# A hybrid attention encoder on one core: the weight sums of x's first chunk in order of use

## The chip, the cores and the metric

The kernel runs on one core of a Trainium2 chip. The metric is the device time of one execution in microseconds (us), the median of several runs. Lower is better.

## The reference, cut to what matters

Two encoder layers on 512 tokens of width 1024, all in float32. Each layer normalizes x, makes one wide projection, runs attention over the tokens and over 256 memory tokens, gates the result and projects it back:

```python
for i in range(DEPTH):
    h = rmsnorm(x, norm_g[i])
    mem_h = rmsnorm(mem, mem_norm_g[i])
    proj = jnp.einsum('bsd,de->bse', h, w_in)          # w_in_a or w_in_b
    ...
    o_mem = memory_attention(q_mem, mem_h, w_mem_kv[i], mem_qn_g[i], mem_kn_g[i])
    y = jnp.concatenate([o_mix, o_mem], axis=-1) * jax.nn.silu(gate)
    x = x + jnp.einsum('bse,ed->bsd', y, w_out[i])
```

Nearly all the work is in the projections, whose weights (some 140 MB with the parts that are read twice) stream in from HBM.

## The kernel before, in words

**The products.** A large projection is cut into *chunks* of weight columns, and each chunk is computed by a Winograd form of Strassen's scheme: seven products instead of eight, at the price of sums of activation blocks and of weight blocks. Each product takes one or two weight tiles of 128x1024 (the index `x` in the code). In the order in which TensorE uses them (`ORDER`) the weight operands of a chunk are `21`, `11`, `T1`, `T2`, `22`, `T3`, `T4`. `21`, `11` and `22` are loaded as they are. The four sums are made on the chip: T1 = `12` + `11`, T2 = `22` + T1, T3 = `12` + `22`, T4 = `21` + T2.

**From a loaded tile to a product.** SyncE issues the loads (`Weights.dma`, L265), as many ahead as the budget of live tiles (`KEEP`, `KEEP_C`) lets it. The sums are drawn in `Weights.sum`. T1 is a VectorE add (L283) for most chunks; for the chunks that `by_dma` names, of which x's first chunk (index 0 in `PLAN`, the first that multiplies the normalized x; two chunks of memory keys and values come before it) is the one that matters here, it is a DMA issued by GpSimd that reads `11` again from HBM and adds it into the tile (L279). T2 (L288), T3 (L293) and T4 (L298) are adding DMAs from GpSimd too; T2 and T4 add one SBUF tile to another, T3 adds `22` from HBM. Products of float32 are made of three products of a rounded high part and a low part: ScalarE casts the high part `wh` (L314), VectorE subtracts for the low part `wo` (L324), and TensorE runs L174 and L175 with `wh` and L178 with `wo`. The operand ring holds four tiles.

**What sets the order.** The program's order is fixed while it is recorded. After each group of matmuls `Weights.advance` counts `g` up by one, records the subtractions, then draws at most one sum, the casts and the loads. `sum` goes through the first eight of its list, which stands in `ORDER`, and draws the first that is *ripe*: its load and the sum that it needs were recorded at least `LEAD` = 2 groups ago (one for some). A sum that isn't ripe is passed over. T1 of x's first chunk is also held back until `g` is `T1_AT` = 7. An engine works strictly in its recorded order: a DMA issue on GpSimd whose load hasn't landed holds all that stands behind it on GpSimd.

**What else stands in these queues.** GpSimd makes the factors of the norms: L495, L453 and L454 turn sums of squares into `rstd`, L663 scales it for the memory keys (`mem_kv`). VectorE multiplies with them (L604 makes `xn`, L500 normalizes x), TensorE transposes the products (L611, L506; L1096 for the memory queries of chunk 3). In `setup` SyncE loads the rope tables (L980 to L983, of which `grA` is a small one), VectorE scales them (L985 to L989), GpSimd multiplies them out (L992). Results leave PSUM by L389 (ScalarE) and L406 (VectorE); those of chunk 0 are stored by L1067 to `v0d`. Chunk 3 follows chunk 0, then chunk 4.

Of the kernel before, what the change touches and what calls it, by code (L numbers as in the profile page):

```python
# [24 lines left out]
BULK, ACTIVE, SET_AT, T1_AT, MEM_B, PREP_Y, PREP_B, HALF, SET_B = 2, 2, 15, 7, 14, 1, 1, {"a": 3, "b": 3, "o": 0}, 9  # L25
# [104 lines left out]
def trunk_kernel(ctx: ExitStack, tc: tile.TileContext, x, mem, wall, norm_g, mem_norm_g, gcol,  # L130
# [63 lines left out]
    def by_dma(c):  # L194

        return c == T1_DMA[0] or c >= T1_DMA[1]

    class Weights:
        def __init__(self):
            self.items, self.last, self.need, self.allocs, self.sums = [], [], [], [], []  # L200
            self.users, self.kinds = {}, []
            g = 0
            for c in SEQ:
                kind, d = PLAN[c], sum(pieces(k) for k in PLAN[:c])
                base = len(self.items)
                if kind in GROUPS:
# [20 lines left out]
                else:  # L227
# [3 lines left out]
                    for k in ORDER:  # L231
                        for x in range(n):
# [7 lines left out]
                            g += 1  # L240
                self.kinds += [kind] * (g - len(self.kinds))
            assert sum(pieces(k) for k in PLAN) == wall.shape[0]
            self.g = -1
            self.live = 0
# [25 lines left out]
        def sum(self, force=False, want=None):  # L270

            for n, (key, d) in enumerate(self.sums[:8]):
                if want and key != want:
                    continue
                c, k, x = key
                if k == "T1" and by_dma(c):
                    if not self.ripe(self.load_at, key, force) or self.g < T1_AT and not force:
                        continue
                    G.dma_start(self.tile[key], wall[d], accum_op=ALU.add)  # L279
                elif k == "T1":  # L280
                    if not (self.ripe(self.load_at, key, force) and self.ripe(self.at, (c, "11", x), force)):
                        continue
                    V.tensor_tensor(self.tile[key], self.tile[key], self.tile[c, "11", x], ALU.add)  # L283
                    self.use((c, "11", x))
                elif k == "T2":
                    if not (self.ripe(self.load_at, key, force) and self.ripe(self.at, (c, "T1", x), force, 1 if c < T1_DMA[1] else None)):
                        continue
                    G.dma_start(self.tile[key], self.tile[c, "T1", x], accum_op=ALU.add)  # L288
                    self.use((c, "T1", x))
                elif k == "T3":  # L290
                    if not self.ripe(self.load_at, key, force):
                        continue
                    G.dma_start(self.tile[key], wall[d], accum_op=ALU.add)  # L293
                else:
                    if not (self.ripe(self.lo_at, (c, "21", x), force, 1) and self.ripe(self.at, (c, "T2", x), force, T4_AT.get(c))):
                        continue
                    self.tile[key] = self.tile[c, "21", x]
                    G.dma_start(self.tile[key], self.tile[c, "T2", x], accum_op=ALU.add)  # L298
                    self.use((c, "T2", x))
                self.at[key] = self.g  # L300
                self.sums.pop(n)
                return True
            return False
# [1362 lines left out]
```

## Time and profile before

| | before |
|---|---|
| median of 3 runs | 959.22 us (958.16 to 960.2) |
| the profiled execution: its own time | 958.25 us |
| its span in the trace | 956.5 us |
| TensorE busy | 940.2 us (98%) |
| VectorE, ScalarE, GpSimd busy | 788.8, 679.6, 339.3 us |
| DMA: moved, mean rate | 204.55 MB, 214 GB/s |
| granted TensorE clock, mean | 0.996 |

TensorE's busy time is near the span, so the other engines matter where TensorE waits for them. In the page's rows, `L12` is line 12 of the kernel, `out<-in` are the program's names for tiles (`wl` a weight tile, `wh` and `wo` its high and low part, `pj` a PSUM tile), and the bracket at a row's end is the idle time of the engine before it and who ended it. A DMA issue appears on the engine that issues it (POOL is GpSimd, SPq is SyncE's queue); its transfer goes on afterwards on the 16 DMA engines, which all queues share.

### The profile page before, as it was taken

What the parts mean: (1) busy time and instruction counts of PE and PEld (TensorE: products, weight loads), DVE (VectorE), ACT (ScalarE), POOL (GpSimd) and SP (SyncE); (2) the same over time, 40 slices, a digit from 0 to 9 for tenths busy, and PEclk for the clock granted to TensorE, in tenths of its full rate; (3) what the DMA queues carried; (4) which work ended last, traced back from release to release, by engine and by line L of the source; (5) the groups of instructions that cost most, each with busy time, mean ns of one, the idle gap of its engine ahead of it and who ended that gap; (6) DMA issues with size and microseconds to landing.
All of it is one profiled execution on the core that took longest, in us unless ns stands there. A gap on an engine that the chain in (4) does not pass through costs nothing.

```text
span 956.5 us, 16572 instructions
## 1 busy us (share of the span) xinstructions
PE 940.2 (98%) x5680; PEld 833.1 (87%) x5680; DVE 788.8 (82%) x1411; ACT 679.6 (71%) x1696; POOL 339.3 (35%) x486
## 2 busy tenths in 40 slices
PE   8799999999999999999999999999899999999998
PEld 6688988888888888888889998888899999998886
DVE  6599676788888897979788999877988898779982
ACT  7565689786868676777676668547778977878860
POOL 3323422647454646373746111213232340111110
PEclk9899999999999999999999999999999999999999
DMA  9999936969786969696877979979966687786524
GB/s 349 362 248 322 290 114 162 311 133 253 158 262 155 263 156 255 147 244 144 228 184 199 278 195 249 288 239 317 245 156 133 194 233 181 206 206 184 119 61 129
DMA packets 86486, 204.55 MB, mean 214 GB/s; under 512 B 25089, under 2 KB 34561, under 8 KB 86402
## 3 DMA queue, kind: packets, MB, share of 16 engines
q1 hardware_dynamic: 66962, 139.46, 42.6%
q0 software_dynamic: 18144, 61.87, 34.9%
q10 hardware_dynamic: 1296, 2.16, 0.6%
q8 instruction: 45, 0.74, 0.3%
q14 instruction: 39, 0.32, 0.1%
HBM read 157.52 MB, written 11.34 MB: 177 GB/s over the span
## 4 chain that ended last, share of the span: by engine, by line
PE 89%; DMA 4%; DVE 3%; ACT 2%; issue 1%; POOL 1%; SPq 0%; DVEq 0%; POOLq 0%; ACTq 0%
PE pj L175 23%; PE pj L174 23%; PE pj L178 23%; PE qT L611 2%; DMA wl<-in_wall_dram 2%; PE sa L1186 1%; PE oo L1294 1%; PE pt L1273 1%; PE ptb L1496 1%; PE sa L1182 1%; DVE wo L324 1%; DMA x<-in_x_dram 1%; PE ob L178 1%; PE ob L175 1%; PE ob L174 1%
## 5 line engine op out<-in xcount | busy, mean ns | idle before, releaser
L324 DVE TENSOR_TENSOR wo<-wl,wh 128x1024 fp32r<-128x1024 f32 x255 | 315.7, 1244 | 6.0 <-ACT wh L314 5.7
L314 ACT CAST wh<-wl 128x1024 fp32r<-128x1024 f32 x255 | 268.6, 1060 | 33.3 <-PE pj L175 19.2
L174 PE MATMUL pj<-wh,hS 128*128 128x512 f32 (+1 forms) x448 | 157.4, 365 | 0.8 <-DVE sn L406 0.8
L175 PE MATMUL pj<-wh,hS 128*128 128x512 f32 (+1 forms) x448 | 152.3, 353 | 0.6 <-DVE hS L575 0.6
L174 PE MATMUL pj<-wh,h 128*128 128x512 f32 (+1 forms) x336 | 118.9, 367 | 0.0
L175 PE MATMUL pj<-wh,h 128*128 128x512 f32 (+1 forms) x336 | 115.2, 356 | 1.1 <-DVE h L575 1.1
L454 POOL TENSOR_TENSOR rstd<-mse,half 128x4 f32<-128x4 f32 (+2 forms) x96 | 101.3, 1056 | 8.0
L178 PE MATMUL pj<-wo,hS 128*128 128x512 f32 (+1 forms) x448 | 100.1, 353 | 0.0
L175 PEld LDWEIGHTS pj<-wh,hS 128*128 128x128 f32 x448 | 85.0, 190 | 11.1 <-DVE hS L575 0.8
L174 PEld LDWEIGHTS pj<-wh,hS 128*128 128x128 f32 x448 | 84.8, 189 | 11.1 <-DVE sn L406 1.2
L178 PEld LDWEIGHTS pj<-wo,hS 128*128 128x128 f32 x448 | 74.6, 189 | 12.2 <-DVE wo L324 0.4
L453 POOL TENSOR_SCALAR mse<-hss 128x4 f32<-128x4 f32 (+1 forms) x86 | 43.2, 503 | 112.1 <-ACT junk L599 107.8
L599 ACT ACTIVATE junk<-sn 128x128 f32<-128x128 f32 x264 | 79.1, 308 | 2.2 <-DVE sn L400 2.2
L389 ACT COPY sn<-pj 128x512 f32<-128x512 f32 x116 | 64.5, 590 | 21.6 <-PE pj L178 20.8
L1130 POOL TENSOR_TENSOR ta<-sn,tabs 128x128 f32<-128x128 f32 (+1 forms) x64 | 35.4, 561 | 118.2 <-DVE sn L604 91.2
L178 PE MATMUL pj<-wo,h 128*128 128x512 f32 (+1 forms) x336 | 75.6, 355 | 0.0
L175 PEld LDWEIGHTS pj<-wh,h 128*128 128x128 f32 x336 | 64.3, 191 | 8.9 <-DVE h L575 1.3
L174 PEld LDWEIGHTS pj<-wh,h 128*128 128x128 f32 x336 | 64.2, 191 | 7.4
L406 DVE TENSOR_TENSOR sn<-pj,sn 128x512 f32<-128x512 f32 x87 | 59.6, 686 | 8.5 <-PE pj L178 8.1
L298 POOL DMA_DIRECT2D wl<-wl x33 | 29.2, 896 | 104.4 <-DVE wo L324 49.4
L178 PEld LDWEIGHTS pj<-wo,h 128*128 128x128 f32 x336 | 56.6, 191 | 9.0
L288 POOL DMA_DIRECT2D wl<-wl x33 | 30.9, 960 | 66.3 <-DMA wl<-in_wall_dram 11.4
(252 smaller groups left out, 2361.3 us busy)
## 6 DMA issues: line engine op xcount, KB each, us to landing
wl<-in_wall_dram SPq DMA_DIRECT2D x222, 512.0 KB, 7.3
wl<-wl POOLq DMA_DIRECT2D x66, 512.0 KB, 5.6
wl<-in_wall_dram POOLq DMA_DIRECT2D x44, 512.0 KB, 8.5
od<-o SPq DMA_DIRECT2D x11, 256.0 KB, 5.4
og<-od SPq DMA_DIRECT2D x10, 256.0 KB, 8.6
x<-in_x_dram SPq DMA_DIRECT2D x4, 512.0 KB, 9.0
v0d<-sn SPq DMA_DIRECT2D x8, 256.0 KB, 6.0
acc<-in_x_dram POOLq DMA_DIRECT2D x8, 256.0 KB, 6.1
```

Source lines behind the costliest of these rows:

```text
L174: T.matmul(o, a, b, start=start, stop=False, skip_group_check=True)
L175: T.matmul(o, c, d, start=False, stop=False, skip_group_check=True)
L178: T.matmul(o, a, b, start=False, stop=stop, skip_group_check=True)
L288: G.dma_start(self.tile[key], self.tile[c, "T1", x], accum_op=ALU.add)
L314: A.copy(wh, self.tile[self.items[i]])
L324: V.tensor_tensor(wo, self.tile[key], wh.bitcast(F32), ALU.subtract)
L389: A.copy(t, b)
L406: V.tensor_tensor(t, b, t, ALU.subtract if q == "12" else ALU.add)
L453: G.tensor_scalar(e, ss, EPS, None, ALU.add)
L454: G.tensor_tensor(r, e, half[:, 0:n], ALU.pow)
L599: A.activation(jk, p[:, j * 128:(j + 1) * 128], AF.Square, scale=by, accum_out=ss[:, j:j + 1])
L1130: G.tensor_tensor(ta[:, 0:n], xn[:, 0:n, 0:32], ropeA[:, 0, b, s0:s0 + n], ALU.mult)
```

## The change

```diff
                 c, k, x = key
                 if k == "T1" and by_dma(c):
-                    if not self.ripe(self.load_at, key, force) or self.g < T1_AT and not force:
+                    if self.g < T1_AT and not force:
+                        break
+                    if not self.ripe(self.load_at, key, force):
                         continue
                     G.dma_start(self.tile[key], wall[d], accum_op=ALU.add)
```

While T1 of x's first chunk is held back (`g` below 7), the search now ends there, and nothing behind it in the list is drawn. Before, T1 was passed over and T3, whose load was old enough, was drawn ahead of it. The last chunks that `by_dma` names come long after `g` = 7, so nothing changes there. All line numbers behind the change are two higher.

What moves is small. On GpSimd, at the end of the memory keys and the beginning of chunk 0, there stood before (L495, L453, L454 is the norm of x's fourth block, L663 the factor of the second block of memory keys, L293 T3's sum, L279 T1's, L288 T2's, L298 T4's):

```order
L454 TENSOR_TENSOR rstd<-mse,half 128x4
L293 DMA wl<-in_wall_dram 128x1024
L495 TENSOR_TENSOR mse<-ss 128x1
L453 TENSOR_SCALAR mse<-mse 128x1
L454 TENSOR_TENSOR rstd<-mse,half 128x1
L663 TENSOR_SCALAR rstd<-rstd,rm 128x4
L293 DMA wl<-in_wall_dram 128x1024
L279 DMA wl<-in_wall_dram 128x1024 x2
L288 DMA wl<-wl 128x1024 x2
L298 DMA wl<-wl 128x1024 x2
```

And now:

```order
L456 TENSOR_TENSOR rstd<-mse,half 128x4
L497 TENSOR_TENSOR mse<-ss 128x1
L455 TENSOR_SCALAR mse<-mse 128x1
L456 TENSOR_TENSOR rstd<-mse,half 128x1
L665 TENSOR_SCALAR rstd<-rstd,rm 128x4
L281 DMA wl<-in_wall_dram 128x1024 x2
L290 DMA wl<-wl 128x1024 x2
L295 DMA wl<-in_wall_dram 128x1024 x2
L300 DMA wl<-wl 128x1024 x2
```

T3's two issues went from ahead of and between the norm's factors to behind T2's. On VectorE one instruction moves, in the second half of chunk 0's products: the add of chunk 3's T1 (L283). There stood before, between the low parts (L324) and the activation's low parts (L575):

```order
L324 TENSOR_TENSOR wo<-wl,wh 128x1024
L283 TENSOR_TENSOR wl<-wl 128x1024
L324 TENSOR_TENSOR wo<-wl,wh 128x1024
L575 TENSOR_TENSOR h_717<-f_478,h_717 128x4x128
L575 TENSOR_TENSOR hS_666<-fS_589,hS_666 128x4x128
L324 TENSOR_TENSOR wo<-wl,wh 128x1024 x2
L575 TENSOR_TENSOR h_717<-f_555,h_717 128x4x128
```

And now:

```order
L326 TENSOR_TENSOR wo<-wl,wh 128x1024 x2
L577 TENSOR_TENSOR h_715<-f_476,h_715 128x4x128
L577 TENSOR_TENSOR hS_664<-fS_587,hS_664 128x4x128
L326 TENSOR_TENSOR wo<-wl,wh 128x1024
L285 TENSOR_TENSOR wl<-wl 128x1024
L326 TENSOR_TENSOR wo<-wl,wh 128x1024
L577 TENSOR_TENSOR h_715<-f_553,h_715 128x4x128
```

The add went behind two more low parts of chunk 0 and two of the activation. TensorE, ScalarE and SyncE keep their order.

## Prediction

> **What bounds the kernel now.** I read the page first. TensorE is busy nearly all the time, and the DMA engines are full for the first five slices (some 120 us) and then nearly idle for one.
>
> ```profile
> span 956.5 us, 16572 instructions
> PE 940.2 (98%) x5680; PEld 833.1 (87%) x5680; DVE 788.8 (82%) x1411; ACT 679.6 (71%) x1696; POOL 339.3 (35%) x486
> DMA  9999936969786969696877979979966687786524
> ```
>
> So the end is set by TensorE's own stream, and only a stop of TensorE is worth anything. The timeline of TensorE over the first 130 us has one such stop; these are the rows around it (start, length, engine, line).
>
> ```profile
> 33.38 0.60 PE L611 MATMUL qT<-ident,xn 128*128 128x128 f32 x4
> 35.68 1.08 PE L178 MATMUL pj<-wo,act 128*128 128x512 f32 x4
> 42.80 1.09 PE L611 MATMUL qT<-ident,xn 128*128 128x128 f32 x4 [6.04 <-DVE xn L604]
> 47.10 1.83 PE L178 MATMUL pj<-wo,h 128*128 128x512 f32 x4
> 57.81 0.39 PE L174 MATMUL pj<-wh,hS 128*128 128x512 f32 x1
> ```
>
> TensorE waits 6.04 us for VectorE's xn (the last row, the first product with T1's weights, is used below). The timelines of VectorE and GpSimd say who held that up.
>
> ```profile
> 30.02 0.08 DVE L491 DVE_READ_ACCUMULATOR2_ANT ss<- 128x1 f32 x1
> 41.96 0.69 DVE L604 TENSOR_TENSOR xn<-pj,rstd 128x512 f32<-128x512 f32 x1 [9.33 <-POOL rstd L663]
> 29.67 1.33 POOL L454 TENSOR_TENSOR rstd<-mse,half 128x4 f32<-128x4 f32 x1
> 39.34 1.07 POOL L293 DMA_DIRECT2D wl<-in_wall_dram  x1 [8.34 <-DMA wl<-in_wall_dram]
> 40.18 0.47 POOL L495 TENSOR_TENSOR mse<-ss 128x1 f32<-128x1 f32 x1
> 41.62 0.30 POOL L663 TENSOR_SCALAR rstd<-rstd,rm 128x4 f32<-128x4 f32 x1
> 42.52 2.07 POOL L279 DMA_DIRECT2D wl<-in_wall_dram  x2
> ```
>
> GpSimd was free at 31.0 (29.67 + 1.33) and the input of L495 was there at 30.1, but L293, the issue of T3's first sum, stood in front and waited for its load until 39.3. The whole chain L495 to L663, then VectorE, then TensorE, stood behind it.
>
> **What the change removes.** In the changed order GpSimd has no DMA issue before L663. L495 to L663 takes 41.92 - 40.18 = 1.74 us, so L663 ends at about 31.0 + 1.8 = 32.8, not 41.9, and xn at 33.5. TensorE ends its group at 36.76 (35.68 + 1.08), so it doesn't wait: 6.04 us go. There is a second part. The windows give the granted clock:
>
> ```profile
> 36.70:42.80 6.10, 0.06 (x2) 0.04 (x1) 0.84 (x2) 1.97 (x3) 3.29 (x7) 0.92 1.04 390
> 42.80:49.00 6.20, 6.20 (x19) 4.99 (x20) 6.11 (x9) 0.81 (x2) 1.79 (x2) 0.53 1.06 219
> 43.20:48.00 4.80, 4.80 (x15) 3.85 (x14) 4.80 (x7) 0.00 (x0) 1.39 (x2) 0.50 1.06 208
> 71.00:75.00 4.00, 4.00 (x20) 3.30 (x19) 4.00 (x5) 3.92 (x6) 0.00 (x0) 1.00 0.76 225
> 85.00:107.00 22.00, 22.00 (x179) 21.60 (x178) 17.80 (x19) 12.08 (x29) 4.29 (x5) 1.00 1.05 341
> 126.00:144.00 18.00, 18.00 (x104) 15.75 (x103) 14.02 (x23) 15.08 (x45) 4.78 (x8) 1.00 0.23 65
> ```
>
> (The last three columns are granted clock, DMA share, GB/s.) The clock falls late in the stop, and TensorE then runs at 0.53 for 6 us. A transpose and its group took 36.76 - 33.38 = 3.38 us before the stop and 48.93 - 42.80 = 6.13 after it: 2.75 us more. So TensorE gets 6.04 + 2.75 = **8.8 us** ahead by about 40 us.
>
> **What the sums that move cost.** T1's two issues (L279) no longer stand behind T3's and can start at 32.8 instead of 42.5; T2's follow, and T3's come after them. The nearest row to their need is this wait of ScalarE for T2's second sum:
>
> ```profile
> 63.64 1.05 ACT L314 CAST wh<-wl 128x1024 fp32r<-128x1024 f32 x1 [2.52 <-DMA wl<-wl]
> ```
>
> With TensorE 8.8 us early it is needed at 54.9. The chain from the first L279 to that landing lasted 63.6 - 42.5 = 21.1 us; from 32.8 it ends at 53.9. It is in time, by 1 us. Loads now share the engines with the chain, so a delay of 0 to some 3 us is possible; I take none. T3's sums are used after T2's (the order of use is 21, 11, T1, T2, 22, T3, T4), and VectorE's add for chunk 3 (L283) moves behind two low parts of 1.2 us and two shorter ones; its own use comes much later, and I take nothing for either.
>
> **What is late next.** This decides the sum. The share of 1.04 to 1.06 in the windows means that the DMA engines have no free time; only 71 to 75 us shows a gap, 4 x (1 - 0.76) = 1.0 us. The change moves no byte away. So whatever waited for a landing in before between 77 and 124 us cannot get it more than about 1 us earlier, however early TensorE is. Three places wait in order for such landings.
>
> First, VectorE's L989 needs the small table grA.
>
> ```profile
> grA<-in_qn_a_dram SPq DMA_DIRECT2D x1, 48.0 KB, 8.5
> 65.98 0.42 SPq L982 DMA_DIRECT2D grA<-in_qn_a_dram  x1
> 69.16 0.86 POOL L288 DMA_DIRECT2D wl<-wl  x1 [4.16 <-DVE wl L283]
> 69.75 1.17 POOL L293 DMA_DIRECT2D wl<-in_wall_dram  x1
> 77.21 0.20 DVE L989 TENSOR_SCALAR grA<-grA 128x96 f32<-128x96 f32 x1
> 77.93 5.34 DVE L324 TENSOR_TENSOR wo<-wl,wh 128x1024 fp32r<-128x1024 f32 x2
> 85.32 1.23 DVE L283 TENSOR_TENSOR wl<-wl 128x1024 f32<-128x1024 f32 x1 [2.05 <-DMA wl<-in_wall_dram]
> 86.46 1.22 DVE L324 TENSOR_TENSOR wo<-wl,wh 128x1024 fp32r<-128x1024 f32 x1
> 84.45 1.07 PE L178 MATMUL pj<-wo,h 128*128 128x512 f32 x4
> 90.15 1.12 PE L178 MATMUL pj<-wo,h 128*128 128x256 f32 x8
> ```
>
> The table landed at 65.98 + 8.5 = 74.5. Behind the change, chunk 3's two sums, which GpSimd issued at 69.2 and 69.8, come earlier (the first waits for VectorE's L283, which follows TensorE's pace, less those four VectorE instructions) and get in front of it. A sum moves 0.524 MB at the 208 GB/s of the window 43.2 to 48, where sums run alone: 2.5 us each. So the table lands between 73.5 (the gap of 1.0 used, no sum ahead) and 79.5 (both ahead, no gap used); I take 77.4, nearer to both ahead, less the gap and about 1 us of overlap. VectorE would reach L989 at 77.2 - 8.8 = 68.4 and then stand there until 77.4, about when it got there before. Half of the 5.34 us pair after it is T4's second low part, ready at about 80.8; TensorE used it at 84.45. So TensorE keeps 84.45 - 80.8 = 3.7 us and gives back 5 us in a new wait there.
>
> Second, L283 (chunk 4's first sum) waited for loads that landed at 85.3. Landing 1.0 us earlier, its successor L324 ends at 86.7 instead of 87.7, against TensorE's use at 90.15: 3.5 us stay.
>
> Third, GpSimd at 105 us.
>
> ```profile
> 105.42 0.93 POOL L293 DMA_DIRECT2D wl<-in_wall_dram  x1 [6.71 <-DMA wl<-in_wall_dram]
> 107.12 0.88 POOL L293 DMA_DIRECT2D wl<-in_wall_dram  x1 [0.76 <-DMA wl<-in_wall_dram]
> 108.38 1.05 POOL L454 TENSOR_TENSOR rstd<-mse,half 128x4 f32<-128x4 f32 x1
> 109.47 0.69 DVE L604 TENSOR_TENSOR sn<-sn,rstd 128x512 f32<-128x512 f32 x1 [2.60 <-POOL rstd L454]
> 111.65 0.60 PE L1096 MATMUL qT<-ident,sn 128*128 128x128 f32 x4
> ```
>
> This is the same blockade again, with chunk 4's T3: rstd stands behind L293. VectorE's product ends at 110.16 and TensorE uses it at 111.65, 1.5 us later. With landings 1.0 us earlier, TensorE can keep 1.5 + 1.0 = **2.5 us**. After 126 us the DMA share is 0.23, nothing waits for landings, and what is left should last to the end.
>
> The sum, against the profiled execution of 958.25 us: -8.8, then +5.1 at T4's second low part, +0.2 at L283, +1.0 at L293, so -2.5: 955.75. The median of the three runs is 959.22, 0.97 above the profiled run; so I forecast **956.7**.
>
> **Rivals.** (B) *The clock falls at the new stop.* The removed stop of 6.0 us cost 2.75 us of slow clock; the new one of about 5 us may cost the same. TensorE then keeps 3.7 - 2.75 = 0.95 us, below what GpSimd at 105 us allows: 958.3. For it: the two stops are nearly as long. Against it: the old clock fell only in the last part of the stop (0.92 on average over it), and part of the new stop may be spread over earlier small waits. The Trainium skill, page "TensorE: Matmul & The Clock Gate", section "What's actually happening", says that the clock halves after one idle window of about 3.4 us, and that the window runs freely. By that rule a stop of 5 us halves it in about half of the cases (an estimate from the page: (5.0 - 3.4)/3.4), which would give 958.3 in those and 956.7 in the others; the two windows of 0.92 and 0.53 agree with it.
>
> (C) *More comes through.* If the sums do not get in front of the loads, the table lands at 73.5 and chunk 4's loads 2.5 to 5 us earlier; -4 to at most -8.8: 950.4 to 955.2. Against it speaks the full DMA share over 85 to 107 us.
>
> (D) *Slower: sums overtake loads.* If one more sum of 2.5 us (chunk 3's last, L298) is served before the loads for L283 and no gap is used, L283 starts at 87.8, its L324 ends at 90.2, and TensorE, which used it at 90.15, has gained nothing; the longer stop, over 6 us, also brings 2.75 us of slow clock: 962.0. It decides from a landing at about 86 us on, with the clock down. For it: the sums do move forward in time against the loads. Against it: L298 stands behind the rope table's products on GpSimd, which themselves wait for grA.
>
> **How the numbers follow.** A measurement of this kernel can tell about 0.2%, 1.9 us, from no change. My forecast has 0.45 (of it 0.38 beyond 0.2%), B 0.25 (0.22 within, 0.03 slower by its spread), C 0.12 (all faster), D 0.18 (0.17 slower, 0.01 within). So faster 0.50, same 0.30, slower 0.20. The range 951.5 to 961.5 leaves out the far end of C and the worst of D, less than 0.2 together. The forecast's own range is 955.5 (all 3.7 us stay) to 957.7 (no landing earlier at all, 1.5 us stay).
>
> **What would show it.** Right: TensorE has no wait at 36 to 43 us, and GpSimd's rstd chain (now L497 to L665) ends near 32.8; the group of T1 starts near 49 us instead of 57.8; VectorE idles at the table grA (now L991) for several us and TensorE waits at T4's second low part between 75 and 81 us; GpSimd's L295 ends its wait near 104; TensorE's transpose L1098 stands near 109. A granted clock of about 0.5 in the windows after 80 us means B. Wrong: if the grA table has landed before 72 us or T1's group isn't early, the step on landings or the step on the chain has failed; if VectorE waits at L285 beyond 86 us, it is D.

## The result, and the profile after

| | before | after |
|---|---|---|
| median | 959.0 us (958.02 to 960.24, 15 runs) | 957.83 us (956.68 to 959.4, 15 runs) |
| ratio, 95% interval | | 0.9987 [0.9979, 0.9995] |
| profiled execution, span | 958.25 us, 956.5 us | 958.09 us, 956.2 us |

The changed kernel is 1.2 us faster, 0.13%. The forecast was 956.7 us (0.26%); 957.83 lies in its wide range, and just outside its own range of 955.5 to 957.7.

The page of the changed kernel shows the same instructions and almost the same busy times; only the time between them moved.

```profile
span 956.2 us, 16572 instructions
PE 939.7 (98%) x5680; PEld 832.3 (87%) x5680; DVE 788.6 (82%) x1411; ACT 680.5 (71%) x1696; POOL 339.4 (35%) x486
```

GpSimd's timeline of the changed kernel at the memory keys (start, length, engine, line):

```profile
31.33 0.53 POOL L497 TENSOR_TENSOR mse<-ss 128x1 f32<-128x1 f32 x1
32.81 0.33 POOL L665 TENSOR_SCALAR rstd<-rstd,rm 128x4 f32<-128x4 f32 x1
33.07 2.00 POOL L281 DMA_DIRECT2D wl<-in_wall_dram  x2
```

The factor is done at 33.1 us, where it was 41.9 before, and T1's sums go out behind it. TensorE's timeline shows what came of it. The rows are the transpose that had waited 6.04 us, the first product of T1, the last product ahead of a new wait, the first behind it, the low part of T4's second group (84.45 before), and the transpose that stood at 111.65 before.

```profile
36.95 0.60 PE L613 MATMUL qT<-ident,xn 128*128 128x128 f32 x4
49.22 0.39 PE L174 MATMUL pj<-wh,hS 128*128 128x512 f32 x1
72.85 0.39 PE L175 MATMUL pj<-wh,h 128*128 128x512 f32 x1
78.04 0.80 PE L174 MATMUL pj<-wh,h 128*128 128x512 f32 x1 [4.80 <-DVE sn L408]
83.18 1.07 PE L178 MATMUL pj<-wo,h 128*128 128x512 f32 x4
110.15 0.60 PE L1098 MATMUL qT<-ident,sn 128*128 128x128 f32 x4
```

TensorE reaches T1 at 49.22 where it was 57.81: 8.6 us ahead. At T4's low part it is only 84.45 - 83.18 = 1.27 us ahead, and at 110 us 1.50. Between them stands one wait of 4.80 us, for VectorE's L408. VectorE's timeline says what held L408 up:

```profile
70.18 0.06 DVE L990 MEMSET gk<- 32x3 f32 x1
77.17 0.21 DVE L991 TENSOR_SCALAR grA<-grA 128x96 f32<-128x96 f32 x1 [6.93 <-DMA grA<-in_qn_a_dram]
77.30 0.68 DVE L408 TENSOR_TENSOR sn<-pj,sn 128x512 f32<-128x512 f32 x1
77.90 5.29 DVE L326 TENSOR_TENSOR wo<-wl,wh 128x1024 fp32r<-128x1024 f32 x2
83.12 1.21 DVE L285 TENSOR_TENSOR wl<-wl 128x1024 f32<-128x1024 f32 x1
```

L408 needs only a finished PSUM bank. It stood behind L991, the scaling of a 48 KB table, and VectorE works in order: it stood there for 6.93 us. TensorE's next group needed the bank. The windows (span and length; busy time and count of each engine; then granted clock, DMA share, GB/s) show a second price:

```profile
74.00:77.50 3.50, 0.00 (x0) 0.00 (x0) 0.33 (x2) 0.11 (x1) 0.01 (x1) 1.00 1.05 315
77.60:80.90 3.30, 2.86 (x7) 2.31 (x8) 3.30 (x3) 0.75 (x1) 3.30 (x2) 0.50 1.03 422
81.00:84.00 3.00, 3.00 (x14) 2.44 (x14) 3.00 (x2) 0.81 (x2) 1.56 (x2) 1.00 1.03 406
```

The clock is halved from about 77.6 to 80.9 us (to 80.96 in the trace's clock record), and TensorE works in it from 78.04 on: (80.96 - 78.04)/2 = 1.46 us more. So 4.80 + 1.46 = 6.3 us of the gain are lost at this one place. In this one profiled execution another 1.2 of the 1.5 us left were lost near 867 us, at two short waits in the second layer's attention. The profiles of e6 and e8 below show no such loss there, and the medians, 1.2 us apart, fit the 1.3 to 1.5 us that the changed kernel holds up to that point.

### The profile page after: what moved, and what is told of

Its sections match the earlier page's. It is cut to its first block, busy times and chain, and to the rows that moved or that the text cites. A ratio compares the mean times of both kernels' runs of the same rounds, so it can differ in the third digit from the quotient of the medians.

```text
span 956.2 us, 16572 instructions
## 1 busy us (share of the span) xinstructions
PE 939.7 (98%) x5680; PEld 832.3 (87%) x5680; DVE 788.6 (82%) x1411; ACT 680.5 (71%) x1696; POOL 339.4 (35%) x486
## 4 chain that ended last, share of the span: by engine, by line
PE 84%; DMA 9%; DVE 3%; ACT 2%; issue 1%; POOL 0%; SPq 0%; DVEq 0%; ACTq 0%; POOLq 0%
PE pj L174 22%; PE pj L175 22%; PE pj L178 22%; DMA wl<-in_wall_dram 2%; PE qT L613 2%; DMA grA<-in_qn_a_dram 2%; PE sa L1188 1%; PE oo L1296 1%; PE pt L1275 1%; PE ptb L1498 1%; PE sa L1184 1%; DVE wo L326 1%; DMA x<-in_x_dram 1%; DMA wl<-wl 1%; DMA row<-in_norm_g_dram 1%; DMA odb<-o 1%
## 5 line engine op out<-in xcount | busy, mean ns | idle before, releaser
L175 PEld LDWEIGHTS pj<-wh,hS 128*128 128x128 f32 x448 | 84.9, 190 | 11.1 <-DVE hS L577 0.8
L455 POOL TENSOR_SCALAR mse<-hss 128x4 f32<-128x4 f32 (+1 forms) x86 | 41.3, 481 | 116.5 <-ACT junk L601 112.2
L1132 POOL TENSOR_TENSOR ta<-sn,tabs 128x128 f32<-128x128 f32 (+1 forms) x64 | 38.5, 609 | 117.5 <-DVE sn L606 91.2
L408 DVE TENSOR_TENSOR sn<-pj,sn 128x512 f32<-128x512 f32 x87 | 59.6, 686 | 8.6 <-PE pj L178 8.2
L300 POOL DMA_DIRECT2D wl<-wl x33 | 29.3, 899 | 105.1 <-DVE wo L326 52.9
```

The lines of the kernel that those rows point to most:

```text
L175: T.matmul(o, c, d, start=False, stop=False, skip_group_check=True)
L408: V.tensor_tensor(t, b, t, ALU.subtract if q == "12" else ALU.add)
L455: G.tensor_scalar(e, ss, EPS, None, ALU.add)
L1132: G.tensor_tensor(ta[:, 0:n], xn[:, 0:n, 0:32], ropeA[:, 0, b, s0:s0 + n], ALU.mult)
```

## The experiments

After the result two theories stood against each other. **Bytes:** the prediction's, that the DMA engines have no free time, so that some operand of TensorE is late whatever is done. **Order:** what is lost is lost because VectorE stands, in its fixed order, at an instruction that waits for a landing, while the data of all that is queued behind it is there. "Landing theory" in the expectations means that the gain is lost at the landing that VectorE waits for.

### e1 and e2: the tables later

The tables' loads, their scaling and the products behind it come some 16 groups later; the tables get room in the tile that the mask is loaded to, so the mask's load follows the products. (`yield n` hands on for n groups.) e1 is the changed kernel with this, e2 the kernel before.

```diff
     def setup():
-        nc.sync.dma_start(mask, mask_d)
-        nc.sync.dma_start(tabA, tab_a.rearrange("p (b c d) -> p b c d", b=2, c=4))
-        nc.sync.dma_start(grA[:, 0:3], qn_a[0:1, :, 0:32].to_broadcast([128, 3, 32]))
-        nc.sync.dma_start(grA[:, 3:6], kn_a[0:1, :, 0:32].to_broadcast([128, 3, 32]))
         yield 4
...
         V.memset(gk[0:32, :], 1.0)
+        yield 12
+        nc.sync.dma_start(tabA, tab_a.rearrange("p (b c d) -> p b c d", b=2, c=4))
+        nc.sync.dma_start(grA[:, 0:3], qn_a[0:1, :, 0:32].to_broadcast([128, 3, 32]))
+        nc.sync.dma_start(grA[:, 3:6], kn_a[0:1, :, 0:32].to_broadcast([128, 3, 32]))
+        yield 4
         V.tensor_scalar(grA[:, 0:3], grA[:, 0:3], QS, None, ALU.mult)
```

> The changed kernel, with the loads of the small rope tables and of the mask, their scaling on VectorE and the products on GpSimd moved some 16 groups later, to where the DMA engines are nearly idle. Landing theory (the 8.6 us won at the norm are given back because VectorE stands at the table's landing while the DMA engines are full): the 4.8 us stop of TensorE goes, VectorE next stands at chunk 4's first sum until about 79 to 81 us, TensorE has a stop of 0 to 2 us there and no half clock, and 5.5 to 8 us of the gain last: ratio to the kernel before 0.9915 to 0.9945. Rival (bytes, not places: any full DMA time is paid somewhere): the stop only moves to chunk 4's first sum or to GpSimd's T3 of chunk 4, ratio 0.997 to 0.999.

> The kernel before with the same later tables, so with the norm's factors still behind T3's issue. Landing theory: before had no stop of TensorE between 44 and 130 us, so the tables hid nothing there and moving them gains nothing: ratio 0.999 to 1.001. Rival (the tables cost TensorE time by themselves, whatever the order of the sums): ratio below 0.997.

e1: 956.87 us (5 runs), ratio 0.9970 [0.9958, 0.9982]. e2: 959.41 us (11 runs), 1.0001 [0.9992, 1.0009]. e2 gained nothing, as expected: without the change the tables cost nothing there. In e1 the wait at the table is gone, but VectorE stands elsewhere; here are its row, TensorE's row and a window of e1:

```profile
83.13 1.23 DVE L285 TENSOR_TENSOR wl<-wl 128x1024 f32<-128x1024 f32 x1 [9.93 <-DMA wl<-in_wall_dram]
```

```profile
85.55 1.57 PE L178 MATMUL pj<-wo,h 128*128 128x256 f32 x8 [3.42 <-DVE wo L326]
```

```profile
86.30:89.50 3.20, 2.87 (x14) 2.61 (x13) 3.20 (x5) 0.32 (x1) 0.87 (x1) 0.50 0.79 248
```

VectorE now waits 9.93 us at the next instruction that needs a landing, chunk 4's first add, until 83.13 us where the landing theory had 79 to 81; TensorE waits for the low part behind it, and the clock halves again. The time is what the rival expected ("the stop only moves"). This does not yet tell the theories apart: the stop moved to another instruction of VectorE, and that may be bytes or order.

### e3: fewer bytes

The changed kernel, with two adding DMAs of chunk 3 not issued (its operands T2 and T3 lack a term).

```diff
                 elif k == "T2":
...
-                    G.dma_start(self.tile[key], self.tile[c, "T1", x], accum_op=ALU.add)
+                    if c != 3:
+                        G.dma_start(self.tile[key], self.tile[c, "T1", x], accum_op=ALU.add)
...
                 elif k == "T3":
...
-                    G.dma_start(self.tile[key], wall[d], accum_op=ALU.add)
+                    if c != 3:
+                        G.dma_start(self.tile[key], wall[d], accum_op=ALU.add)
```

> The changed kernel without the two DMA sums T2 and T3 of chunk 3 (left out, so the products of chunk 3 use the wrong weights): two times 2.5 us of DMA work less in front of the table. Landing theory: the table lands at about 72 instead of 77.2, VectorE stands there some 2 us instead of 6.9, TensorE's stop of 4.8 us falls under 1 us, the clock stays up, and 6 to 8 us of the gain last: ratio 0.9915 to 0.994. Rival (the stop is set by something else than the DMA engines' load, such as the issue of the table's load on SyncE): table and stop stay where they are, ratio 0.998 to 0.9995.

952.37 us (4 runs), 0.9924 [0.9911, 0.9937]. With two sums fewer on the DMA engines the table's wait on VectorE shrinks from 6.93 to 2.45 us and ends 4.5 us earlier (77.17 before this edit):

```profile
72.62 0.21 DVE L993 TENSOR_SCALAR grA<-grA 128x96 f32<-128x96 f32 x1 [2.45 <-DMA grA<-in_qn_a_dram]
```

So the sums do stand in front of the table's load, as the prediction had it, and when the landings come earlier most of the gain stays (7.1 us). Both theories allow that.

### e4: is it the norm, or the order of use?

The kernel before, with T3 of x's first chunk held back until the norm's factor is recorded, but still drawn ahead of T1.

```diff
                 elif k == "T3":
-                    if not self.ripe(self.load_at, key, force):
+                    if not self.ripe(self.load_at, key, force) or c == 0 and self.g < T1_AT - 1 and not force:
                         continue
```

> The kernel before with T3 of chunk 0 held back just until the norm's factors are recorded: T3's first sum still goes ahead of T1's, but no longer stands in front of the norm. Landing theory: the stop of 6 us at the norm goes all the same; T1 is about 7 us later than in the changed kernel, TensorE stops 2 to 5 us at T1 or T2 in pieces, but as the table lands at about 77 us in any case the stop there shrinks by as much: the end is that of the changed kernel within 1.5 us, ratio 0.997 to 0.9995. Rival (the order of use of the sums is what counts): 2 to 4 us slower than the changed kernel, ratio 1.001 to 1.003.

958.29 us (12 runs), 0.9986 [0.9977, 0.9994], beside 0.9987 of the change. The equal times are not equal causes, though. GpSimd's timeline of e4 shows the factor done early and T3's blockade now behind it, but ahead of T1's sums:

```profile
33.75 0.33 POOL L663 TENSOR_SCALAR rstd<-rstd,rm 128x4 f32<-128x4 f32 x1
40.47 1.08 POOL L293 DMA_DIRECT2D wl<-in_wall_dram  x1 [6.40 <-DMA wl<-in_wall_dram]
41.30 2.07 POOL L279 DMA_DIRECT2D wl<-in_wall_dram  x2
```

The norm's stop is gone without the new order of the sums. But T1's sums go out at 41.3 instead of 33.1, and T1's tile reaches ScalarE at 53.06, behind an idle time of 5.96 us; a PSUM tile's copy (L389) stands behind that cast, and TensorE waits for it. ScalarE's row and TensorE's:

```profile
53.06 1.04 ACT L314 CAST wh<-wl 128x1024 fp32r<-128x1024 f32 x1 [5.96 <-DMA wl<-in_wall_dram]
```

```profile
55.16 0.79 PE L174 MATMUL pj<-wh,hS 128*128 128x512 f32 x1 [4.83 <-ACT sn L389]
```

So e4 loses at T1 what the change loses at the table. Whether the order of use is worth something by itself only a kernel without the later loss can tell: e11, below.

### e5, e6 and e7: chunk 4's add later as well

The add that held e1 up is recorded only when its load is six groups old instead of two. e5 is e1 with this, e6 the changed kernel with this alone, e7 the kernel before with both.

```diff
                 elif k == "T1":
-                    if not (self.ripe(self.load_at, key, force) and self.ripe(self.at, (c, "11", x), force)):
+                    if not (self.ripe(self.load_at, key, force, 6 if c == 4 else None) and self.ripe(self.at, (c, "11", x), force)):
                         continue
```

> The changed kernel with the rope tables loaded, scaled and multiplied later, as in e1_tables_late, and with VectorE's add for chunk 4's T1 held back until its load is six groups old, so that neither the small table nor chunk 4's load is waited for by VectorE in its order. Theory (the gain is lost because VectorE stands in its fixed order at a landing, while the products behind it have their data): no stop of TensorE over 3 us before 120 us, no half clock after 36 us, TensorE 7 us or more ahead of before at 90 us, 7.0 to 8.3 us faster than before: ratio 0.991 to 0.993. Rival (the DMA engines have no free time, so some other operand is late by as much): the stop only moves again, 3 us or more of it, with half clock behind it: ratio 0.995 to 0.998.

> The changed kernel with only VectorE's add for chunk 4's T1 held back, the tables where they were. Both theories put the stop of this kernel at the scaling of the small table, ahead of that add, so both expect it to stay: a TensorE wait of 4 to 6 us near 78 us, half clock behind it, and the time of the changed kernel within 0.1%: ratio 0.998 to 0.9995 against before. If the ratio falls below 0.996, the add was the bound and the table only stood near it.

> The kernel before with the same two edits as e5_tables_and_add_late. Both theories: its stop of 6 us at the norm is untouched and nothing else stops TensorE by more than 1 us there, so no gain: ratio 0.999 to 1.001. A ratio below 0.998 would say that the two edits bring time by themselves and e5 is no measure of what the change is worth.

| | median | ratio, 95% |
|---|---|---|
| e5 | 950.82 us (4 runs) | 0.9912 [0.9897, 0.9927] |
| e6 | 957.93 us (10 runs) | 0.9988 [0.9977, 0.9998] |
| e7 | 959.36 us (10 runs) | 1.0003 [0.9993, 1.0012] |

In e5 TensorE has no wait above 0.9 us from the norm to 130 us. In e6 the table's wait stays, as both theories said; TensorE's row and two windows:

```profile
78.79 0.51 PE L174 MATMUL pj<-wh,h 128*128 128x512 f32 x1 [4.32 <-DVE sn L408]
```

```profile
78.80:79.10 0.30, 0.30 (x1) 0.29 (x2) 0.30 (x1) 0.00 (x0) 0.30 (x1) 1.00 1.07 437
79.20:82.50 3.30, 3.30 (x9) 2.54 (x8) 3.30 (x2) 1.04 (x1) 3.30 (x2) 0.50 1.03 415
```

e7 keeps the norm's wait, and with it the time of before:

```profile
43.68 1.08 PE L611 MATMUL qT<-ident,xn 128*128 128x128 f32 x4 [6.34 <-DVE xn L604]
```

So the two edits are worth nothing without the change and 7 us with it (0.9987 - 0.9912): they bring back what the change had freed. This speaks for order, but e5 also moves loads, so bytes could still have a part.

### e8, e9 and e10: the waiting instructions moved, the loads not

e8 is the changed kernel in which no load and no adding DMA is moved by hand; L991 (with the products behind it) is recorded four groups later, and chunk 4's add on VectorE is held as in e5. (An adding DMA that stood behind those products on GpSimd does go out earlier; more of it at e9.) e9 has the first of these two moves alone, e10 is the kernel before with both.

```diff
         V.memset(gk[0:32, :], 1.0)
+        yield 4
         V.tensor_scalar(grA[:, 0:3], grA[:, 0:3], QS, None, ALU.mult)
```

> The changed kernel with all loads and sums where they are, and only the instructions that wait moved: the scaling of the small table and the products behind it are recorded four groups later, and chunk 4's add is held as in e5_tables_and_add_late. No transfer is ordered otherwise by hand. Theory of the fixed order: the data of the products is there, only the queue behind the table's scaling was late; the stop at 78 us goes and most of the 8 us stays: ratio 0.991 to 0.995. Rival (bytes): TensorE's own operands are late by as much once nothing stops it, so a stop of 3 us or more with half clock comes elsewhere before 100 us: ratio 0.996 to 0.999.

> The changed kernel with the scaling of the small table and the products behind it four groups later, as in e8_waits_late_loads_not, and chunk 4's add left where it was. Theory of the fixed order: VectorE comes to that add near 74 us and stands there for its load, which lands between 82 and 85 us, so TensorE stops for 3.5 to 5 us and half clock follows; the gain of e8 is lost again though the table no longer holds anything: ratio 0.996 to 0.998. Rival (the table's place alone was the bound): no such stop, ratio 0.990 to 0.993.

> The kernel before with the two moves of e8_waits_late_loads_not. Theory: before, neither instruction stops TensorE, and the stop of 6 us at the norm stays, so nothing is gained: ratio 0.999 to 1.001, a TensorE wait of about 6 us at the transpose of xn and half clock behind it. Rival: the moves bring time by themselves, and the 9.3 us of e8 are not those of the norm: ratio below 0.998, and by as much as it is below 1 the part of e8 that is not the change's.

| | median | ratio, 95% |
|---|---|---|
| e8 | 949.91 us (4 runs) | 0.9904 [0.9889, 0.9919] |
| e9 | 960.42 us (10 runs) | 1.0014 [1.0004, 1.0023] |
| e10 | 959.14 us (10 runs) | 1.0004 [0.9994, 1.0013] |

e8 is the best of all: 9.3 us faster than before, a little more than its theory expected, by an edit that removes no byte. (The spans of the profiled executions, 956.5 and 947.9 us, are 8.6 apart.) VectorE's timeline of e8 shows both instructions met by data that is there (no bracket), and TensorE's the transpose of 111.65 now at 103.04, 8.6 us ahead:

```profile
78.47 0.20 DVE L992 TENSOR_SCALAR grA<-grA 128x96 f32<-128x96 f32 x1
84.84 1.23 DVE L285 TENSOR_TENSOR wl<-wl 128x1024 f32<-128x1024 f32 x1
```

```profile
103.04 0.60 PE L1099 MATMUL qT<-ident,sn 128*128 128x128 f32 x4
```

e9 lies outside both expectations: slower than before, although the norm is free. It is the same add that decides. Its rows on VectorE, then TensorE, then the windows:

```profile
85.28 1.23 DVE L285 TENSOR_TENSOR wl<-wl 128x1024 f32<-128x1024 f32 x1 [11.66 <-DMA wl<-in_wall_dram]
91.63 0.20 DVE L992 TENSOR_SCALAR grA<-grA 128x96 f32<-128x96 f32 x1
```

```profile
87.70 2.08 PE L178 MATMUL pj<-wo,h 128*128 128x256 f32 x8 [5.15 <-DVE wo L326]
95.50 0.39 PE L174 MATMUL pj<-wh,hS 128*128 128x256 f32 x1 [2.28 <-DVE sn L408]
113.03 0.60 PE L1099 MATMUL qT<-ident,sn 128*128 128x128 f32 x4
```

```profile
87.40:90.70 3.30, 3.00 (x13) 2.92 (x14) 3.30 (x6) 1.04 (x1) 0.87 (x1) 0.50 0.82 260
90.80:95.00 4.20, 2.42 (x20) 2.21 (x19) 4.20 (x5) 1.53 (x2) 3.08 (x3) 1.00 0.92 266
```

VectorE stands 11.66 us at the add. TensorE waits 5.15 us, then works 3 us at half clock; meanwhile VectorE is busy without a gap (3.30 of 3.30, 4.20 of 4.20) with what had piled up, and TensorE catches up with it and waits another 2.28 us. That second wait is what the expectation had left out. Sum: 5.15 + 2.28 + some 1.5 = 8.9 us, more than the 7.8 us that TensorE was ahead; at the transpose it is 113.03 against 111.65. e9 and e8 differ only in where that one add stands (and in what follows from it), and by 10.5 us.

The landing that the add waits for also came later than in the changed kernel. There chunk 3's first T4 sum (L300) stands on GpSimd behind the table's products, which wait for L991. In e9 these products are recorded later, and the sum goes out 9.4 us earlier. GpSimd's rows of the changed kernel and of e9:

```profile
83.55 0.89 POOL L300 DMA_DIRECT2D wl<-wl  x1 [1.44 <-DVE wo L326]
```

```profile
74.19 0.87 POOL L300 DMA_DIRECT2D wl<-wl  x1 [6.83 <-DVE wo L326]
```

In the changed kernel the add's load was issued at 73.74 and landed 8.6 us later, at 82.4. In e9 it was issued at 74.12 and took 11.1 us, to 85.2. The 2.8 us between them fit one sum of 2.5 us (the prediction's figure) that was served first; no run moves that sum alone. In e8 the sum also goes out early (73.64), and the load lands at 84.75. VectorE is done with the low part ahead of the add at 84.82, so e8 meets its data there by less than 0.1 us.

e10 shows that the two moves are nothing by themselves; the norm's wait is there:

```profile
43.64 1.07 PE L611 MATMUL qT<-ident,xn 128*128 128x128 f32 x4 [5.31 <-DVE xn L604]
```

### e11: the order of the sums by itself

e4's edit and e8's two moves together, made on the kernel before: the norm is free, nothing waits behind T1, and only T3 still goes ahead of T1.

> e4_t3_first_behind_norm (the norm is free, T3's sum is still drawn ahead of T1's) with the two moves of e8_waits_late_loads_not, so that nothing behind T1 takes the gain away. Theory: the order of the sums counts by itself; T3's blockade keeps T1's first sum until 53 us as in e4, TensorE waits 4 to 5 us at T1 near 55 us with half clock behind it, and some 7 us of 8.6 are gone before the table is reached: ratio 0.997 to 1.001. Rival: freeing the norm is all that counts and e4's wait at T1 only stood where another would have: ratio 0.990 to 0.993, as e8.

956.30 us (8 runs), 0.9971 [0.9961, 0.9982], as the theory had it. TensorE's row:

```profile
55.26 0.50 PE L174 MATMUL pj<-wh,hS 128*128 128x512 f32 x1 [4.69 <-ACT sn L389]
```

e8 differs from e11 in the order of T1, T2 and T3 alone (and, through it, in where VectorE's add for chunk 3 stands), and is 0.9971 - 0.9904 = 0.0067 lower, 6.4 us.

**What follows.** In this kernel the loss is one of order: e8 keeps every byte and keeps the gain. Bytes still set when a landing comes (e3, and the load in e9). The change does two things: it frees the norm (e4 has that), and it gets T1's sum out in time (e11 lacks that, and keeps only 2.5 us). T1's order with the norm still blocked was not run. Together they free 8.6 us. Its own kernel loses 6.3 of them at one instruction of VectorE that now comes to a landing too early, and behind it a second such instruction stood ready to do the same.

## Why the prediction was right, and where it was wrong

**The norm's chain: right.** The text had L665 end near 32.8, and T1 near 49 us; it was 33.1 and 49.22. The gain of 8.8 us there measured 8.6. That T1's sums start at once behind the norm was in the text as part of T2's chain; that 6.4 us hang on it once the norm is free (e11) was not.

**T2's second sum: in time by 1 us, it said; late by 0.8.** ScalarE's row of the changed kernel:

```profile
56.16 1.06 ACT L316 CAST wh<-wl 128x1024 fp32r<-128x1024 f32 x1 [3.94 <-DMA wl<-wl]
```

The chain from L281 at 33.07 took 23.1 us, not the 21.1 of before, since loads now run beside it. TensorE waited 0.79 us for the low part at 60.25. The text named a delay of 0 to 3 us and took none.

**First place, the small table: right in cause and landing, too cheap.** VectorE came there at 70.2 and left at 77.2 (68.4 and 77.4 in the text). But TensorE was stopped one group earlier than predicted. The text looked for who uses the low part behind the table's scaling, and overlooked that the emptying of a PSUM bank stands there too. In the kernel before it is this row (L408 in the changed kernel):

```profile
77.33 0.68 DVE L406 TENSOR_TENSOR sn<-pj,sn 128x512 f32<-128x512 f32 x1
```

And the stop brought half clock: 4.80 + 1.46 = 6.3 us lost in place of 5.1. This was rival B's mechanism. B priced the clock at 2.75 us where it cost 1.46. With the 0.8 us lost at T2, TensorE kept 1.27 us at T4's second group, near B's 0.95 and far from the 3.7 of the forecast.

**The step that failed: "whatever waited for a landing in before between 77 and 124 us cannot get it more than about 1 us earlier".** In the changed kernel the landings at the other two places came much earlier. L285 starts at 83.12 without a wait: its load landed at 82.4, where it had come at 85.2 before. And GpSimd's blockade at 105 us moved by 3.5 us at its first issue (105.42 before, 101.95 after, where the text had "near 104") and by 3.8 at its second (107.12 and 103.37), not by 1.0:

```profile
101.95 0.92 POOL L295 DMA_DIRECT2D wl<-in_wall_dram  x1 [4.86 <-DMA wl<-in_wall_dram]
103.37 0.87 POOL L295 DMA_DIRECT2D wl<-in_wall_dram  x1 [0.49 <-issue]
105.38 0.23 POOL L455 TENSOR_SCALAR mse<-hss 128x4 f32<-128x4 f32 x1 [1.14 <-ACT junk L601]
```

Behind them GpSimd waits 1.14 us for ScalarE, that is for TensorE's pace; the place that should have set "2.5 us" set nothing, and in e8 TensorE passes it 8.6 us ahead. (In e8 the held add also changes the order of GpSimd's sums there, so this place was not tried by itself.) The total of -2.5 against a measured -1.2 came as near as it did by luck: two faults went against each other, a first place that was too cheap, and a bound behind it that wasn't one.

Why the bound wasn't one: the text took a DMA share above 1 to mean that each landing is fixed in time. But the same share moves different amounts. The windows of before and after from 75 to 80 us:

```profile
75.00:80.00 5.00, 5.00 (x24) 4.14 (x23) 4.97 (x10) 1.39 (x2) 2.50 (x2) 1.00 1.06 282
```

```profile
75.00:80.00 5.00, 1.96 (x5) 1.59 (x6) 2.83 (x3) 0.00 (x0) 2.51 (x2) 0.75 1.04 383
```

From 80 to 85 us it is 339 GB/s at 1.04 before and 411 at 1.03 after, so 0.9 MB more landed in these 10 us at the same share. The adding DMAs are the slow part: where they run alone the prediction's window has 208 GB/s at 1.06, and with plain loads the window from 30 to 36 us of before has 410 at 1.03. In the changed kernel chunk 3's second sum had landed by 77.0 us, against 83.5 before, and loads took the rest of the stretch.

And loads had room to be late. The window of e8 that holds the same 104 matmuls as 126 to 144 us of before shows it:

```profile
117.40:135.40 18.00, 18.00 (x104) 15.74 (x103) 14.02 (x23) 15.06 (x45) 4.77 (x8) 1.00 0.44 134
```

The share is 0.44 at 134 GB/s, against 0.23 at 65 in before: 18 us x 69 GB/s = 1.2 MB, more than two weight tiles, that had landed before that stretch of TensorE's work now land in it, and TensorE does not wait there (busy 18.00 of 18.00). Some of the loads before 124 us were ahead of their use. The Trainium skill, page "Perfetto Trace Analysis", section "Identifying the Most-Contended Engine", says to judge the DMA engines by how much of HBM's bandwidth is used, because with 16 engines their occupancy misleads. The windows of the changed kernel agree as far as that goes: shares of 1.05 and 1.03 stand beside 315 and 422 GB/s.

**The rivals.** B came true in half: the clock fell, for 3.4 us instead of the 6.8 of before. Its estimate that a stop of 5 us brings this in about half of the cases was low here: all seven kernels with a stop of 3.4 to 5.3 us lost the clock, since a step of TensorE's work need not be quite idle for it (last section). C's thesis, that landings are not fixed, was nearer to the truth than the forecast's, but its gain did not come, since VectorE's order stood in between. D did not happen in the changed kernel: the table was late, but chunk 4's loads were not. L300 stood behind the table's products, as the text had said against D. Where it doesn't stand there (e9), the load comes at 85.2, though not at D's 87.8.

## What to carry to other kernels

When a stop goes, look on every engine that TensorE waits for, in recorded order, for the next instruction that needs a DMA's landing, and ask whether the engine now comes to it before the landing: there it stands, and all that is queued behind it is late, ready or not. Such instructions are moved behind work whose data is there; here two of them decided between 0.9904 and 1.0014 with the same first repair. Moving one is not enough while the next stands close behind it, so count what is left after each.

## What the runs showed of the hardware

In the clock records of these traces the half clock behind a stop lasts one or two times 3.41 us and doesn't go by the length of the stop. Stops of 4.80 us (after) and 4.83 us (e4) brought 3.4 and 6.8 us of it, in e4 from 53.8 on; 6.04 (before) and 6.34 (e7) brought 6.8, 5.31 (e10) and 5.15 (e9) 3.4. In e6 it began at 79.15, when TensorE was back at work since 78.79. What fits all of them is that TensorE's busy time in each step of 3.41 us decides. In the step ahead of the fall in e1 TensorE was busy for 0.66 us, and in the first half-clock steps of before and e4 for 2.40 of 3.30 and 1.94 of 3.30, which was not enough to end it:

```profile
82.80:86.20 3.40, 0.66 (x5) 0.66 (x6) 3.07 (x4) 0.63 (x1) 0.00 (x0) 1.00 1.00 402
```

```profile
41.90:45.20 3.30, 2.40 (x8) 2.15 (x9) 3.24 (x5) 0.00 (x0) 2.69 (x4) 0.50 1.06 226
```

```profile
53.80:57.10 3.30, 1.94 (x5) 1.56 (x6) 2.43 (x3) 2.60 (x5) 0.94 (x3) 0.50 0.88 171
```

In the changed kernel 2.86 of 3.30 (the window from 77.6, above) ended it. So a step that is 73% busy keeps the half clock and one of 87% ends it, while a step 19% busy brings it on. The Trainium skill, page "TensorE: Matmul & The Clock Gate", section "What's actually happening", gives a window of 3413 ns that runs freely and decides by how busy TensorE was in it; the lengths and the start in e6 agree.
